# A recorded two-block transformer kernel: exact shapes in its planner, an order by latest start time, and weight slots of 4352 bytes

## The chip, the cores and the metric

The kernel runs on one core of a Trainium2 chip. The metric is the device time of one execution in microseconds, lower is better. TensorE (PE) multiplies, with its weight loads on a path of their own (PEld); VectorE (DVE), ScalarE (ACT) and GpSimd (POOL) do elementwise work; SyncE (SP) starts the DMA transfers. Each engine works off its own list of instructions in order, and waits where an input or a buffer isn't ready.

## The reference, cut to what matters

Two blocks follow one another on 512 tokens of width 1024, in float32.

```python
def reference(x, ...):
    x = first_block(...)     # rmsnorm; h @ w_in; mLSTM, pooling and memory-attention branches, each
                             # times silu of a gate; concatenated @ w_out; rmsnorm
    return second_block(...)

def second_block(...):       # h is 512 x 1024
    p = h @ w_in + b_in
    a_u, a_v, q, k, v, r, a_low, g_a, g_b = split(p)
    y_a = spatial_gating(a_u, a_v, ...)
    log_f = log_sigmoid(a_low @ gla_w_gate2 + gla_b_gate) / 16
    o = gla_chunked(q, k, v, log_f)          # gated linear attention, 4 heads, below
    y_b = normalise(o) * gla_norm_g * silu(r)
    m = sigmoid(g_a) * y_a + sigmoid(g_b) * y_b
    h = layer_norm(alpha * h + m @ w_out)
    f = square(relu(h @ w_ff1)) @ w_ff2      # 1024 -> 4096 -> 1024
    return layer_norm(alpha * h + f)

def gla_chunked(q, k, v, log_f):             # per chunk of 64 tokens, with a state carried over
    cum = cumsum(log_f)
    scores[t, s] = sum_d q[t, d] * k[s, d] * exp(cum[t, d] - cum[s, d])   for s <= t
    out = scores @ v + (q * exp(cum)) @ state
```

## The kernel before, in words

**Weights.** All big products are taken in the format fp32r, with three matmuls in place of one: activations and weights are each split into a high and a low part, and high·high, high·low and low·high are added up in PSUM. The weights come as 184 chunks of 128x1024 numbers or close to it, numbered in the order in which they are used. A chunk n is loaded by an SP DMA into a tile `wr`n; ACT copies it, rounded, into `wh`n; DVE takes the difference `wl`n = `wr`n − `wh`n (`split_to`, L562 to 577). Tiles `wr`, `wh` and `wl` have four buffers each (`RAW, HL = 4, 4`, L541). A chunk then feeds 24 matmuls of 128x512 into one PSUM bank (`fm`, L637, through `mm3`, L506: two with `wh`, one with `wl`, eight times): the weight is the stationary side, and the moving side is a page `pg` of activations (512 tokens x 4 bytes). In eight chunks (56 to 63, the `av` columns) the sides are changed: 48 matmuls whose moving side is 256 columns of the weight (`units_tok`, L650). Some chunks (117 to 123, and most of the second feed-forward matrix) are put into pages `pg` instead of `wh` and `wl`; they are called paged. Inside a chunk the eight input pages are gone through in turn, so the first matmul with `wl` is the third of the chunk.

**Recording and planning.** Nothing is issued when the Python code runs. `Recorder.add` (L142) notes every operation with its tiles and what it depends on; `costs` (L185) gives each a modelled time by its engine, its kind and the number of elements n that its views (`View`, L62) report. `serial` (L236) makes an order in which the tiles fit in their buffers; `order` (L286) is a list scheduler over the five engines: at each step it takes for each engine, among the operations whose inputs are planned, the one that can start first, looking through them in program order, and of the engines' candidates the one with the earliest start. `issue` (L413) then emits everything, so every instruction of the profile carries one line, L431. The last line of the kernel calls `rec.issue(rec.order({...}))`.

A view keeps n exactly only while it is a plain slice. After a `rearrange` followed by an index it reports the n of the whole tile: a 128x4x32 part of a `big` tile of 768 columns is costed with n = 768.

**The GLA stage.** While the chunks from about 82 to 104 (the `q`, `k`, `r` and `ga` columns of the second block's input product) are multiplied, the function `gla` (L1431) lays the attention's work beside them. For each of four heads and each of five levels, DVE and POOL build decayed copies of q and k in `big` and `pg` tiles, PE makes small score products (`score`, L1527, into banks such as `ps751`, `ps752`), and DVE copies their valid triangles out of PSUM with COPY_PREDICATED into one page (such as `pg721`). Beside this, DVE takes each finished chunk out of its PSUM bank (`pg760<-ps750,pg486`: bank plus bias page), applies a product with an activation's result (SCALAR_TENSOR_TENSOR), and makes the next `wl`. So DVE's list mixes three kinds of rows: those that need a PE result, those that prepare the next scores, and the weight splits. In the order rows below, `ps719`, `ps731`, `ps741`, `ps750`, `ps762` and `ps776` are the banks of chunks 93, 94, 95, 96, 97 and 98; the numbers behind the underscores count the recorded rows.

Of the kernel before, what the change touches and what calls it, by code (L numbers as in the profile page):

```python
# [1 line left out]

# [5 lines left out]
F32 = mybir.dt.float32  # L8
F32R = mybir.dt.float32r
# [12 lines left out]
SLOT = 1088  # L22
# [23 lines left out]
class Tile_:  # L46


    def __init__(self, pool, shape, dtype, tag, bufs, nm):
        self.pool, self.shape, self.dtype, self.tag, self.bufs, self.nm = pool, list(shape), dtype, tag, bufs, nm  # L50
        self.real = None
        self.psum = tag == "ps"
        n = 1
        for s in shape[1:]:
            n *= s
        self.cols = n
        self.writes, self.reads = [], []
        self.first = self.last = None
        self.left = 0


class View:  # L62
    def __init__(self, tile, steps=(), lo=0, hi=None, flat=None, rows=None, n=None, dt=None):
        self.tile, self.steps = tile, steps
        self.lo, self.hi = lo, tile.cols if hi is None else hi
        self.flat = len(tile.shape) == 2 if flat is None else flat
        self.rows = tile.shape[0] if rows is None else rows
        self.n = self.hi - self.lo if n is None else n
        self.dt = tile.dtype if dt is None else dt

    def _next(self, step, **kw):
        a = dict(lo=self.lo, hi=self.hi, flat=self.flat, rows=self.rows, n=self.n, dt=self.dt)
        a.update(kw)
        return View(self.tile, self.steps + (step,), **a)

    def __getitem__(self, ix):
        step = ("getitem", (ix,), {})
        whole = ix if isinstance(ix, tuple) else (ix,)
        if self.flat and all(isinstance(s, slice) and s.step is None for s in whole):
            rows = len(range(*whole[0].indices(self.rows)))  # L80
            lo, hi = self.lo, self.hi
            if len(whole) > 1:
                a, b, _ = whole[1].indices(self.hi - self.lo)
                lo, hi = self.lo + a, self.lo + b
            return self._next(step, lo=lo, hi=hi, rows=rows, n=hi - lo)
        return self._next(step, flat=False)

    def bitcast(self, dt):
        return self._next(("bitcast", (dt,), {}), dt=dt)

    def rearrange(self, p, **kw):
        return self._next(("rearrange", (p,), kw), flat=False)

    def unsqueeze(self, i):
        return self._next(("unsqueeze", (i,), {}), flat=False)

    def to_broadcast(self, shape):
        n = 1
        for s in shape[1:]:
            n *= s  # L100
        return self._next(("to_broadcast", (shape,), {}), flat=False, n=n)

    def real(self):
        ap = self.tile.real
# [25 lines left out]
class Recorder:  # L130
# [54 lines left out]
    def costs(self, o):  # L185

        kw, eng = o.kw, o.eng
        out = kw["out"]
        n = out.n if isinstance(out, View) else 512
        ins = [v for k, v in kw.items() if isinstance(v, View) and k not in WRITES]  # L190
        ps = any(v.tile.psum for v in ins)
        o.port, o.table, o.tail = False, None, 60
        if eng == "PE":
            o.tail = 230
            if o.what == "transpose":
                o.cost = 112
            else:
                n = kw["rhs"].n
                slow = kw["rhs"].dt == F32
                o.cost = 2 * max(112, 0.85 * n) if slow else max(113, 0.449 * n)  # L200
        elif eng == "ACT":
            extra = sum(isinstance(kw.get(k), View) for k in ("scale", "bias"))
            o.cost = (150 if ps else 190) + 0.835 * n + 95 * extra + (206 if "accum_out" in kw else 0)
            fn = kw["func"].name if hasattr(kw["func"], "name") else str(kw["func"]).rsplit(".", 1)[-1]
            o.table = EXACT.get(fn)
        elif eng == "DVE":
            n = max(n, max((v.n for v in ins), default=0))
            ptr = any(isinstance(kw.get(k), View) for k in ("scalar", "scalar1", "scalar2"))
            big = [k for k in ("in_", "in0", "in1", "data", "mask", "data0", "data1") if isinstance(kw.get(k), View)]
            sb = [k for k in big if not kw[k].tile.psum]  # L210
            o.port = len(sb) >= 2 or (len(sb) == 1 and len(big) == 1 and o.what in ("tensor_copy", "tensor_scalar"))
            o.cost = 140 + 1.045 * n + 65 * ptr
            if o.what == "memset":
                o.cost = 50 + n
            elif o.what == "tensor_scalar" and not ps and n >= 256:
                o.cost = 140 + 0.55 * n + 65 * ptr
            elif o.what == "copy_predicated":
                o.cost = 150 + 1.15 * n
            elif o.what == "tensor_tensor_scan":
                o.cost = 1800  # L220
            elif n <= 16:
                o.cost = 210
        elif eng == "POOL":
            o.port = o.what != "memset"
            o.cost = 190 + 2.15 * n
            if o.what == "memset":
                o.cost = 515
            elif o.what == "affine_select":
                o.cost = 260 + 0.75 * n
            elif o.what == "tensor_copy":  # L230
                o.cost = 200 + 1.3 * n
        else:
            o.cost = 440
            o.tail = 2100
# [48 lines left out]
                t.last = i  # L283
        self.ops = order

    def order(self, caps, window=1 << 30):  # L286
        import heapq
        import numpy as np
        self.serial(caps)
        ops = self.ops  # L290
        n = len(ops)
        tags = list(caps)
# [16 lines left out]
        pend = {e: [] for e in engines}  # L309
        for o in ops:  # L310
            o.waiting, o.ready, o.start = len(o.deps), 0.0, None
        for o in ops:
            if not o.waiting:
                heapq.heappush(pend[o.eng], o.i)
        head = 0
        port = 0.0
        wire = 0.0
# [44 lines left out]
        done = 0  # L362
        order = []
        while done < n:
# [6 lines left out]
            pend[e].remove(i)  # L371
            cost = o.cost
            if o.table and table not in o.table:
                table = o.table[0]
# [25 lines left out]
            for j in o.users:  # L400
                u = ops[j]
                u.ready = max(u.ready, o.end if u.eng != e else s + cost + (0 if e != "SP" else o.end - s - cost))
                u.waiting -= 1
                if not u.waiting:
                    pend[u.eng].append(j)
            while head < n and ops[head].start is not None:
                head += 1
            order.append(i)
# [35 lines left out]
def tile_two_blocks(ctx, tc, wa, wb, xT, memT, vec, cst, rows, poolw, wst, wg2, out):  # L444
    ctx.enter_context(tc.manual_schedule())
    rec = Recorder(tc.nc)
# [115 lines left out]
    def split_to(i):  # L562
        while n_sp[0] <= min(i, NCH - 1):
            c = n_sp[0]
            t = raw.pop(c)
            n = src[c].shape[1]
            if c in paged:
                h, l = Pair(), Pair()
                for i in range(2):
                    split(h.pages[i], l.pages[i], t[:, i * T:(i + 1) * T])  # L570
            else:
                h = rec.tile(sb, [128, n], F32R, tag="wh", name=f"wh{c}", bufs=HL)
                l = rec.tile(sb, [128, n], F32R, tag="wl", name=f"wl{c}", bufs=HL)
                split(h, l, t)
            wsp[c] = (h, l)
            n_sp[0] += 1
# [159 lines left out]
    first = []  # L736
    if True:
# [8 lines left out]
            G.memset(f(b), 0.0)  # L746

        for c in range(2):
            first.append([rec.tile(sb, [128, 1040], dt, tag=tag, name=f"{tag}{c}", bufs=n)
                          for tag, dt, n in (("wr", F32, RAW), ("wh", F32R, HL), ("wl", F32R, HL))])  # L750
            wsp[c] = first[c][1:]
        for k in range(8):
            s = slice((k % 4) * 260, (k % 4 + 1) * 260)
# [1384 lines left out]
```

## Time and profile before

| | us |
|---|---|
| time, median of 3 runs (lowest to highest) | 1162.99 (1160.61 to 1163.28) |
| the profiled execution's own time | 1163.84 |
| its span, first to last instruction | 1161.7 |
| PE busy | 1132.3 |
| DVE busy | 706.0 |
| ACT busy | 514.8 |
| POOL busy | 183.3 |
| mean granted TensorE clock over the span | 0.990 |

The span is the time between the first and the last instruction in the trace; the execution's own time is 2.1 us longer. A busy time is the sum over an engine's instructions with overlaps taken out. The granted clock is TensorE's clock as a share of full speed. In the profile, times on the axis are microseconds from the span's start.

### The profile page before, as it was taken

To read this page: it belongs to the slowest core of one execution; us is meant where nothing else is said; L and a number is where in the kernel's file an instruction comes from. 1 tells how busy PE (TensorE), PEld (TensorE's weight loads), DVE (VectorE), ACT (ScalarE), POOL (GpSimd) and SP (SyncE) were. 2 spreads that over 40 slices of the span, in tenths; PEclk is the share of its full clock that TensorE was granted. 3 is DMA by queue.
4 is the path that set the end of the run, shared out by engine and by line. 5 is a ranking of instruction groups with operands and counts; after the bars stand their busy time and mean duration, and the time that the engine had idled before them with its cause. 6 is when DMAs were issued, how large, how long until landed. Compare 5 with 4: busy or idle time off the path is not lost.

```text
span 1161.7 us, 15202 instructions
## 1 busy us (share of the span) xinstructions
PE 1132.3 (97%) x5808; PEld 957.3 (82%) x5808; DVE 706.0 (61%) x1291; ACT 514.8 (44%) x868; POOL 183.3 (16%) x244
## 2 busy tenths in 40 slices
PE   8999999999999999999998899998999999999997
PEld 8888888878889998888876777898888888888885
DVE  6878887886445665565665887887333336423334
ACT  7766535453334525854554343446232226222211
POOL 5112002000120000432444533001000000000005
PEclk9999999999999999999998999999999999999998
DMA  8324222522323222220221131340222223324201
GB/s 300 110 91 174 72 75 80 163 92 93 104 76 110 75 91 71 95 91 19 73 91 37 55 116 66 101 142 31 72 90 93 91 96 105 108 92 156 79 1 72
DMA packets 33799, 108.85 MB, mean 94 GB/s; under 512 B 3888, under 2 KB 5040, under 8 KB 33728
## 3 DMA queue, kind: packets, MB, share of 16 engines
q1 hardware_dynamic: 33728, 107.90, 27.8%
q8 instruction: 45, 0.74, 0.3%
q14 instruction: 26, 0.21, 0.1%
HBM read 105.79 MB, written 2.10 MB: 93 GB/s over the span
## 4 chain that ended last, share of the span: by engine, by line
PE 96%; DVE 3%; ACT 0%; DMA 0%; issue 0%; SPq 0%; DVEq 0%
PE ps L431 96%; DVE pg L431 1%; DVE wl L431 1%; DVE big L431 0%; DMA wr<-in_wb_dram 0%; ACT wh L431 0%; ACT pg L431 0%; DVE sm L431 0%; SPq L431 0%; DVEq L431 0%
## 5 line engine op out<-in xcount | busy, mean ns | idle before, releaser
L431 PE MATMUL ps<-pg,wh 128*128 128x512 f32 (+1 forms) x1952 | 602.7, 391 | 0.9 <-ACT wh L431 0.9
L431 PEld LDWEIGHTS ps<-pg,wh 128*128 128x128 f32 x1952 | 363.1, 189 | 77.7 <-ACT wh L431 1.3
L431 PE MATMUL ps<-pg,wl 128*128 128x512 f32 (+1 forms) x976 | 378.9, 389 | 7.9 <-DVE wl L431 7.7
L431 ACT ACTIVATE wh<-wr 128x1024 fp32r<-128x1024 f32 (+2 forms) x159 | 163.1, 1026 | 338.8 <-PE ps L431 300.6
L431 DVE TENSOR_TENSOR wl<-wr,wh 128x1024 fp32r<-128x1024 f32 (+1 forms) x151 | 189.6, 1258 | 160.9 <-ACT wh L431 160.8
L431 PE MATMUL ps<-pg,pg 128*128 128x512 f32 (+4 forms) x1280 | 241.1, 344 | 3.4 <-DVE pg L431 2.0
L431 PEld LDWEIGHTS ps<-pg,pg 128*128 128x128 f32 (+1 forms) x1280 | 207.4, 192 | 33.5 <-DVE pg L431 2.6
L431 PEld LDWEIGHTS ps<-pg,wl 128*128 128x128 f32 x976 | 184.3, 189 | 50.5 <-DVE wl L431 10.6
L431 POOL TENSOR_TENSOR pg<-pg,pg 128x128 f32<-128x128 f32 (+4 forms) x113 | 111.5, 995 | 654.1 <-ACT pg L431 565.4
L431 ACT ACTIVATE pg<-pg 128x512 fp32r<-128x512 f32 (+6 forms) x254 | 133.0, 550 | 106.4 <-DVE pg L431 91.7
L431 PE MATMUL ps<-wh,pg 128*128 128x260 f32 (+2 forms) x800 | 170.2, 308 | 5.4 <-ACT wh L431 5.4
L431 DVE TENSOR_TENSOR pg<-ps,pg 128x512 f32<-128x512 f32 (+4 forms) x153 | 95.1, 630 | 82.0 <-PE ps L431 76.5
L431 DVE TENSOR_TENSOR pg<-pg,pg 128x512 f32<-128x512 f32 (+7 forms) x207 | 124.2, 623 | 32.1 <-ACT pg L431 14.0
L431 PEld LDWEIGHTS ps<-wh,pg 128*128 128x128 f32 x800 | 130.6, 191 | 12.8 <-ACT wh L431 5.4
L431 PE MATMUL ps<-wl,pg 128*128 128x260 f32 (+2 forms) x400 | 121.3, 305 | 0.0
L431 PEld LDWEIGHTS ps<-wl,pg 128*128 128x128 f32 x400 | 76.0, 190 | 3.9 <-issue 0.5
L431 DVE TENSOR_TENSOR pg<-wr,pg 128x512 fp32r<-128x512 f32 x62 | 40.8, 689 | 61.8 <-issue 41.5
L431 ACT ACTIVATE pg<-wr 128x512 fp32r<-128x512 f32 x62 | 35.4, 623 | 83.4 <-PE ps L431 75.7
L431 DVE SCALAR_TENSOR_TENSOR pg<-pg,pg 128x512 f32<-128x512 f32 (+3 forms) x76 | 51.4, 693 | 4.7 <-ACT pg L431 4.2
L431 ACT ACTIVATE pg<-ps 128x512 f32<-128x512 f32 (+5 forms) x78 | 39.8, 529 | 21.1 <-PE ps L431 20.3
L431 ACT ACTIVATE pg<-pg,vt 128x512 f32<-128x512 f32 (+3 forms) x60 | 39.0, 655 | 10.9 <-DVE pg L431 9.9
L431 DVE SCALAR_TENSOR_TENSOR pg<-pg,vt,pg 128x512 fp32r<-128x512 f32 (+4 forms) x48 | 37.3, 788 | 5.8 <-ACT pg L431 5.0
(131 smaller groups left out, 537.6 us busy)
## 6 DMA issues: line engine op xcount, KB each, us to landing
wr<-in_wa_dram SPq DMA_DIRECT2D x172, 512.0 KB, 3.5
wr<-in_wb_dram SPq DMA_DIRECT2D x10, 520.0 KB, 3.5
pg<-in_xT_dram SPq DMA_DIRECT2D x16, 256.0 KB, 4.1
pg<-in_rows_dram SPq DMA_DIRECT2D x10, 256.0 KB, 4.1
out_dram<-pg SPq DMA_DIRECT2D x8, 256.0 KB, 2.0
wr<-in_wb_dram SPq DMA_DIRECT2D x8, 130.0 KB, 4.0
pg<-in_memT_dram SPq DMA_DIRECT2D x4, 256.0 KB, 7.4
pg<-in_wst_dram SPq DMA_DIRECT2D x2, 256.0 KB, 3.9
```

What stands on the lines that cost most here:

```text
L431: getattr(real[o.eng], o.what)(**kw)
```

## The change

**Exact shapes.** `View` carries its `shape` through indexing, `rearrange`, `unsqueeze` and broadcasts, and n is worked out from it. The modelled costs of the DVE's and POOL's parts of the GLA stage change with it. Three cost constants change too.

**The planner's priority.** `order` now runs the scheduler (`schedule`, the old loop) six times. The first time the priority is program order as before. After each round, `latest` walks the plan backwards and gives each operation the latest time at which it can start without delaying the plan's end, through the operations that use its result, and through PE's own sequence of that plan; the next round looks through candidates by that time. The plan with the earliest modelled end is issued.

**The weight slots.** All `wh` and `wl` tiles get `SLOT` = 1088 columns, 4352 bytes (before 1040 columns, 4160 bytes, the largest of the tiles that share the slots). Chunks of the kinds `km` (4 chunks), the eight `av` chunks and chunk 116 are put 16, 48 and 16 columns into their slot.

The built programs have the same instructions for computing: 5808 recorded matmuls and transposes on PE, 1291 on DVE, the same table loads on ACT. By the addresses in the built programs, `wh` starts 177952 bytes into a partition in both; `wl` starts at 194592 before and 195360 now; the pages `pg` start at 30240 and are 2048 bytes apart. Modulo 256 all pages stand at 32. The four slots of `wh` and of `wl` stand at 32, 96, 160 and 224 before (4160 = 16·256 + 64) and all at 32 now (4352 = 17·256).

```diff
     def __getitem__(self, ix):
...
+        shape = []
+        for k, d in enumerate(self.shape):
+            if k >= len(whole):
+                shape.append(d)
+            elif isinstance(whole[k], slice):
+                shape.append(len(range(*whole[k].indices(d))))
...
-        return self._next(step, flat=False)
+        return self._next(step, flat=False, shape=shape)
...
             elif o.what == "copy_predicated":
-                o.cost = 150 + 1.15 * n
+                o.cost = 160 + 1.1 * n
             elif o.what == "tensor_tensor_scan":
-                o.cost = 1800
+                o.cost = 1200
             elif n <= 16:
-                o.cost = 210
+                o.cost = 165
...
-    def order(self, caps, window=1 << 30):
+    def order(self, caps, rounds=6):
+
+
+        self.serial(caps)
+        got = None
+        prio = [float(o.i) for o in self.ops]
+        for _ in range(rounds):
+            order = self.schedule(caps, prio)
+            if got is None or self.end < got[0]:
+                got = self.end, order, [(o.start, o.end) for o in self.ops]
+            prio = self.latest()
...
+    def latest(self):
+        ops = self.ops
+        end = self.end
+        seq = sorted(ops, key=lambda o: -o.start)
+        late = [end] * len(ops)
+        pe = end
+        pos = {o.i: k for k, o in enumerate(seq)}
+        for o in seq:
+            t = end
+            for j in o.users:
+                t = min(t, late[j] - (o.cost if ops[j].eng == o.eng else o.cost + o.tail))
+            t = min(t, end - o.cost)
+            if o.eng == "PE":
+                t = min(t, pe - o.cost)
+                pe = t
+            late[o.i] = t
+        return late
+
+    def schedule(self, caps, prio):
...
-            for i in sorted(pend[e]):
-                if i > head + window:
-                    break
+            for _, i in pend[e]:
...
+    shift = {4 + i: 16 for i, w in enumerate(ORDER1) if w[0] == "km"}
+    shift.update({4 + len(ORDER1) + 12 + i: 48 for i in range(8)})
+    shift[4 + len(ORDER1) + 12 + 16 + len(ORDER2) + 4] = 16
...
-                h = rec.tile(sb, [128, n], F32R, tag="wh", name=f"wh{c}", bufs=HL)
-                l = rec.tile(sb, [128, n], F32R, tag="wl", name=f"wl{c}", bufs=HL)
+                o = shift.get(c, 0)
+                h = rec.tile(sb, [128, SLOT], F32R, tag="wh", name=f"wh{c}", bufs=HL)[:, o:o + n]
+                l = rec.tile(sb, [128, SLOT], F32R, tag="wl", name=f"wl{c}", bufs=HL)[:, o:o + n]
```

Outside the GLA stage the two orders differ by local swaps. Inside it, two places show the difference.

DVE, GLA stage, before: the rows that lead up to the split of chunk 98.

```order
L431 TENSOR_TENSOR pg746_5839<-pg654_5195,pg746_5839 128x512
L431 COPY_PREDICATED pg721_5616<-ct_180,ps751_5960 128x4x24 x2
L431 COPY_PREDICATED pg721_5616<-ct_180,ps751_5960 128x4x16 x2
L431 COPY_PREDICATED pg721_5616<-ct_180,ps751_5960 128x4x8 x2
L431 COPY_PREDICATED pg721_5616<-ct_180,ps752_5963 128x4x24 x2
L431 COPY_PREDICATED pg721_5616<-ct_180,ps752_5963 128x4x16 x2
L431 COPY_PREDICATED pg721_5616<-ct_180,ps752_5963 128x4x8 x2
L431 TENSOR_TENSOR pg774_6003<-ps762_5914,pg486_3575 128x512
L431 SCALAR_TENSOR_TENSOR pg748_5856<-pg749_5863,pg748_5856 128x512
L431 TENSOR_TENSOR wl98_6008<-wr98_5713,wh98_5799 128x1024
```

DVE, the same place now: the rows that lead up to the split of chunk 98.

```order
L500 TENSOR_TENSOR wl97_5797<-wr97_5493,wh97_5778 128x1024
L500 SCALAR_TENSOR_TENSOR pg729_5782<-pg730_5788,pg729_5782 128x512
L500 TENSOR_TENSOR pg746_5801<-pg654_5207,pg746_5801 128x512
L500 TENSOR_TENSOR pg739_5827<-ps731_5776,pg486_3575 128x512
L500 COPY_PREDICATED pg721_5613<-ct_180,ps732_5823 128x256
L500 COPY_PREDICATED pg721_5613<-ct_180,ps732_5823 128x128
L500 COPY_PREDICATED pg721_5613<-ct_180,ps733_5833 128x256
L500 COPY_PREDICATED pg721_5613<-ct_180,ps733_5833 128x128
L500 TENSOR_TENSOR gsq_5637<-gsq_5637,ps738_5839 4x512
L500 SCALAR_TENSOR_TENSOR pg739_5827<-pg740_5850,pg739_5827 128x512
L500 TENSOR_TENSOR wl98_5872<-wr98_5598,wh98_5825 128x1024
```

Before, `wl98` stood behind the row that reads `ps762`, the bank of chunk 97; now the latest chunk's bank that a row ahead of it reads is `ps731`, that of chunk 94.

PE, GLA stage, before: the end of chunk 96 and what follows it.

```order
L431 MATMUL ps750_5867<-pg462_3347,wh96_5626 128x512
L431 MATMUL ps750_5867<-pg461_3309,wl96_5775 128x512
L431 MATMUL ps762_5914<-pg437_3050,wh97_5758 128x512
L431 MATMUL ps762_5914<-pg438_3057,wh97_5758 128x512
L431 MATMUL ps776_5920<-pg437_3050,wh98_5799 128x512
L431 MATMUL ps776_5920<-pg438_3057,wh98_5799 128x512
L431 MATMUL ps795_5924<-pg437_3050,wh99_5854 128x512
L431 MATMUL ps795_5924<-pg438_3057,wh99_5854 128x512
L431 MATMUL ps762_5914<-pg437_3050,wl97_5933 128x512
L431 MATMUL ps762_5914<-pg439_3062,wh97_5758 128x512
```

PE, the same place now.

```order
L500 MATMUL ps750_5911<-pg462_3347,wh96_5677 128x512
L500 MATMUL ps750_5911<-pg461_3309,wl96_5685 128x512
L500 MATMUL ps751_5969<-big745_5843,pg746_5801 128x192 x2
L500 MATMUL ps752_5978<-big745_5843,pg746_5801 128x192 x2
L500 MATMUL ps762_5986<-pg437_3050,wh97_5778 128x512
L500 MATMUL ps762_5986<-pg438_3057,wh97_5778 128x512
L500 MATMUL ps762_5986<-pg437_3050,wl97_5797 128x512
L500 MATMUL ps762_5986<-pg439_3062,wh97_5778 128x512
```

Before, PE took the first two matmuls of the chunks 97, 98 and 99, those that need no `wl`, ahead of the first `wl97`; now the chunks run whole, one behind the other, with the scores (`ps751`, `ps752`) between two of them.

## Rows read from the trace of the kernel before

**Rows 1.** The page: busy time, share and instructions by engine; chain that ended last.

```profile
PE 1132.3 (97%) x5808; PEld 957.3 (82%) x5808; DVE 706.0 (61%) x1291; ACT 514.8 (44%) x868; POOL 183.3 (16%) x244
...
PE 96%; DVE 3%; ACT 0%; DMA 0%; issue 0%; SPq 0%; DVEq 0%
```

**Rows 2.** PE's waits, whole span: us in total, times, longest us.

```profile
PE ps L431 <- ACT wh L431: 6.3, 2, 5.4
```

**Rows 3.** PE's waits, 551 to 671 us, the GLA stage.

```profile
PE ps L431 <- DVE wl L431: 7.7, 6, 2.6
PE ps L431 <- DVE pg L431: 3.1, 2, 2.0
```

**Rows 4.** Stretches: us; busy (instructions) PE, PEld, DVE, ACT, POOL; PEclk; DMA share; GB/s.

```profile
551.00:580.00 29.00, 27.94 (x136) 23.45 (x135) 20.55 (x63) 16.02 (x37) 11.74 (x18) 1.00 0.22 73
...
610.00:640.00 30.00, 25.41 (x102) 20.15 (x101) 17.67 (x52) 11.96 (x29) 14.40 (x27) 0.89 0.11 36
...
sum 120.00, PE 107.42 PEld 87.61 DVE 83.96 ACT 57.97 POOL 53.90; mean PE 26.86 PEld 21.90 DVE 20.99 ACT 14.49 POOL 13.48
```

**Rows 5.** Timeline, 612 to 632 us: start, us, instruction [idle before, releaser].

```profile
615.40 0.69 DVE L431 TENSOR_TENSOR pg<-ps,pg 128x512 f32<-128x512 f32 x1 [4.29 <-PE ps L431]
616.01 0.68 DVE L431 SCALAR_TENSOR_TENSOR pg<-pg,pg 128x512 f32<-128x512 f32 x1
...
616.61 1.22 DVE L431 TENSOR_TENSOR wl<-wr,wh 128x1024 fp32r<-128x1024 f32 x1
...
617.74 1.73 DVE L431 TENSOR_TENSOR big<-pg,big 128x384 f32<-128x384 f32 x3
...
617.88 0.50 PE L431 MATMUL ps<-pg,wl 128*128 128x512 f32 x1 [1.12 <-DVE wl L431]
...
619.40 0.68 DVE L431 TENSOR_TENSOR pg<-pg,pg 128x512 f32<-128x512 f32 x1
...
622.56 1.75 DVE L431 COPY_PREDICATED pg<-ct,ps 128x96 f32<-128x96 uint32 x12 [2.48 <-PE ps L431]
...
624.69 0.69 DVE L431 TENSOR_TENSOR pg<-ps,pg 128x512 f32<-128x512 f32 x1 [0.38 <-PE ps L431]
...
627.17 0.80 PE L431 MATMUL ps<-pg,wl 128*128 128x512 f32 x1 [2.62 <-DVE wl L431]
...
629.05 1.06 PE L431 MATMUL ps<-pg,wh 128*128 128x512 f32 x2
...
630.33 1.06 PE L431 MATMUL ps<-pg,wh 128*128 128x512 f32 x2
```

**Rows 6.** Stretches of four feed-forward chunks in a row, PE alone.

```profile
882.88:888.32 5.44, 5.44 (x25) 1.00 0.28 96
888.32:893.82 5.50, 5.50 (x25) 1.00 0.30 98
893.82:899.36 5.54, 5.54 (x25) 1.00 0.30 95
899.36:904.91 5.55, 5.55 (x26) 1.00 0.27 94
```

**Rows 7.** Stretches of four `av` chunks, one in each slot, PE alone.

```profile
341.85:347.60 5.75, 5.75 (x50) 1.00 0.01 3
347.60:353.06 5.46, 5.46 (x51) 1.00 0.58 178
377.36:383.06 5.70, 5.70 (x51) 1.00 0.32 99
383.06:388.70 5.64, 5.64 (x50) 1.00 0.30 94
```

**Rows 8.** Stretch of the layer norm behind `w_out`, PE alone.

```profile
788.00:815.00 27.00, 24.58 (x168) 0.87 0.07 21
```

More of the change, by code (lines that the diff above doesn't have):

```diff
@@ L1 @@
+from bisect import insort
 from collections import deque
@@ L62, with __init__ @@
 class View:
-    def __init__(self, tile, steps=(), lo=0, hi=None, flat=None, rows=None, n=None, dt=None):
+    def __init__(self, tile, steps=(), lo=0, hi=None, flat=None, rows=None, shape=None, dt=None):
         self.tile, self.steps = tile, steps
         self.lo, self.hi = lo, tile.cols if hi is None else hi
+        self.shape = tuple(tile.shape) if shape is None else tuple(shape)
         self.flat = len(tile.shape) == 2 if flat is None else flat
         self.rows = tile.shape[0] if rows is None else rows
-        self.n = self.hi - self.lo if n is None else n
+        self.n = 1
+        for d in self.shape[1:]:
+            self.n *= d
         self.dt = tile.dtype if dt is None else dt
     def _next(self, step, **kw):
-        a = dict(lo=self.lo, hi=self.hi, flat=self.flat, rows=self.rows, n=self.n, dt=self.dt)
+        a = dict(lo=self.lo, hi=self.hi, flat=self.flat, rows=self.rows, shape=self.shape, dt=self.dt)
         a.update(kw)
@@ L84, in __getitem__ @@
                 lo, hi = self.lo + a, self.lo + b
-            return self._next(step, lo=lo, hi=hi, rows=rows, n=hi - lo)
-        return self._next(step, flat=False)
+            return self._next(step, lo=lo, hi=hi, rows=rows, shape=shape)
+        return self._next(step, flat=False, shape=shape)
     def bitcast(self, dt):
@@ L91, in rearrange, with groups @@
     def rearrange(self, p, **kw):
-        return self._next(("rearrange", (p,), kw), flat=False)
+        size = dict(kw)
+        left, right = [side.replace("(", " ( ").replace(")", " ) ").split() for side in p.split("->")]
+        def groups(words):
+            got, deep = [], None
+            for w in words:
+                if w == "(":
+                    deep = []
+                elif w == ")":
+                    got.append(deep)
+                    deep = None
+                elif deep is None:
+                    got.append([w])
+                else:
+                    deep.append(w)
+            return got
+        for d, names in zip(self.shape, groups(left)):
+            known, open_ = 1, None
+            for w in names:
+                if w in size:
+                    known *= size[w]
+                else:
+                    open_ = w
+            if open_:
+                size[open_] = d // known
+        shape = []
+        for names in groups(right):
+            d = 1
+            for w in names:
+                d *= size[w]
+            shape.append(d)
+        return self._next(("rearrange", (p,), kw), flat=False, shape=shape)
     def unsqueeze(self, i):
-        return self._next(("unsqueeze", (i,), {}), flat=False)
+        return self._next(("unsqueeze", (i,), {}), flat=False, shape=self.shape[:i] + (1,) + self.shape[i:])
     def to_broadcast(self, shape):
[L98 to L101, printed above, removed]
+        return self._next(("to_broadcast", (shape,), {}), flat=False, shape=shape)
     def real(self):
@@ L284, in serial @@
         self.ops = order
-    def order(self, caps, window=1 << 30):
+    def order(self, caps, rounds=6):
[7 more added lines that the diff above has]
+            prio = self.latest()
+        self.end = got[0]
+        for o, (s, e) in zip(self.ops, got[2]):
+            o.start, o.end = s, e
+        return got[1]
+    def latest(self):
[16 more added lines that the diff above has]
+    def schedule(self, caps, prio):
         import heapq
         import numpy as np
-        self.serial(caps)
         ops = self.ops
@@ L370, in order @@
             o = ops[i]
[L371 removed]
+            pend[e].remove((prio[i], i))
             cost = o.cost
@@ L748, in tile_two_blocks @@
         for c in range(2):
[L749 to L750 removed]
+            first.append([rec.tile(sb, [128, w], dt, tag=tag, name=f"{tag}{c}", bufs=n)
+                          for tag, dt, n, w in (("wr", F32, RAW, 1040), ("wh", F32R, HL, SLOT), ("wl", F32R, HL, SLOT))])
             wsp[c] = first[c][1:]
```

4 lines of the change are left out of this document (2 added, 2 removed).

## Prediction

> **What bounds the kernel now.** I read the page's busy times and its chain first. PE is busy for 1132.3 us of a span of 1161.7, and the chain of waits that ended last is 96% PE and 3% DVE [rows 1]. So there are two ways to gain: take away PE's idle time, some 29 us, or make PE's matmuls themselves follow each other faster. Idle time of the other engines is worth nothing.
>
> Then I asked what PE waits for. 5.4 us are the head, in which the first weight is loaded and split [rows 2]; the change leaves the first rows of SP, ACT and DVE as they were, so that stays. The largest lump behind it lies in the GLA stage, 551 to 671 us. There PE is busy for 107.42 of 120 us: 12.58 us idle [rows 4]. 7.7 of these are six waits for a `wl`, 3.1 two waits for a page that DVE makes [rows 3]. The timeline shows how such a wait comes about. At 615.40 DVE, which had itself waited 4.29 us for PE, takes a finished chunk out of PSUM (0.69), multiplies (0.68), and only then makes the `wl` of the next chunk (1.22), while PE stands still; the same again at 624.69, where PE waits 2.62 us [rows 5]. DVE isn't short of time on the whole (83.96 of 120 us [rows 4]); it waits for PE, and then PE waits for it. The split stands in DVE's list behind the row that reads the chunk before.
>
> The second wait has a sequel: from 627.17 on three matmuls take 1.28 us (629.05 to 630.33 [rows 5]), where 24 take 5.44 in an undisturbed stretch [rows 6], 0.68 for three. The stretch's granted clock is 0.89 [rows 4]: PE ran at 1.2 GHz for a while after the waits. A clock of half for x of 30 us with a mean of 0.89 gives x = 6.6 us, so 3.3 us lost; counted by matmuls, some 13 at 427 ns for 227, it is 2.6.
>
> Last, the pace where PE never waits. Four feed-forward chunks in a row, 24 matmuls each, at full clock and without idle time, take 5.44, 5.50, 5.54 and 5.55 us [rows 6], and each following group of four chunks repeats it. The weight slots are four. The fast one is the slot that stands at 32 modulo 256 like the pages. The `av` chunks show the same kind of thing with other signs: 5.75, 5.46, 5.70 and 5.64 [rows 7].
>
> **Part 1: the slots' pace.** Now all slots stand where the fast one stood. The mean of the four is 5.508, so a chunk gains 0.066 us [rows 6]. 116 chunks have a weight in a slot as stationary side and 512 moving columns: 116 x 0.066 = 7.7 us. The clean stretches are those of the feed-forward part; elsewhere matmuls of other kinds stand between the chunk's own, and fewer neighbours gain. No row gives that share: I take a fifth off, 6.2, and for the low end a third, 5.1. The eight `av` chunks go to what the 5.46 slot has (48 columns are 192 bytes, the same place relative to the pages): mean 5.64 less 5.46, times 8, is 1.4 [rows 7]. The first eight chunks of the second feed-forward matrix also use slots: 8 x 0.066 = 0.5. The four `km` chunks and chunk 116 have no clean row: 0. Sum 8.1, I take **8.0**; ends 5.4 (the low end of the first term, and little from the others) and 9.9 (everything in full, and a few tenths from the `km` chunks). All of it lies on PE, which is the path.
>
> Here the Trainium skill speaks against this part: its page "SBUF — State Buffer", section "Who interferes with whom", gives PE two independent read ports, one for the moving operand and one for the weight load, and says that PE never waits on anyone. By it the place of a slot couldn't matter and this term would be 0. The four stretches differ by up to 2% with the slot alone, so I go by them; the rule is a rival below.
>
> **Part 2: DVE's order in the GLA stage.** I counted for each split how many PE matmuls stand between the latest PE result that a DVE row ahead of it reads and the first matmul that uses it. That is the time by which DVE can be late. Before, it is 0 to 8 for the chunks 89, 97 to 100 and 102. Now it is 93, 88, 90, 65, 65 and 81, the smallest of the stage being 65: at 0.227 us each about 15 us. The order rows show it for chunk 98: behind the bank of chunk 97 before, behind that of 94 now. So the pattern at 615 and 624 us can't come again in that form, and 7.7 us of waits for `wl` and the 3.1 for pages lose their cause.
>
> What is late next is DVE itself. Between `wl98` and `wl99` its list now has six products into `big` (3.5), two bank rows (1.4), 24 copies (3.5 at the rate of the twelve at 622.56), two SCALAR_TENSOR_TENSOR (1.4), one page (0.7) and the split (1.2): 11.7 us [rows 5], against 7 to 8 us of PE for a chunk with its scores. From chunk 98 to 102 this adds up to 47 us of DVE against 32 of PE: DVE falls behind by 15. The lead of `wl102` is 81 matmuls, 18 us. That covers it, with 3 us to spare, less than a tenth of the sum; the tightest score row has a lead of 6 us of PE over 3.4 of DVE. So I keep 2 us of the 12.58 and take **10.6**; ends 0 (the DVE rival) and 12.6.
>
> PE's new order costs nothing by itself: the matmuls are the same in number and kind, and a whole chunk in sequence is what rows 6 show at full pace.
>
> **Part 3: the clock.** Without waits of 1 and 2.6 us some 10 us apart the clock has no cause to fall at 627. I take 2.6, ends 0 and 3.3 [rows 4, 5].
>
> **The rest.** The costs by exact shape, `latest` and the three constants act only through the order. Outside the GLA stage rows are swapped locally. The dearest other place, the layer norm behind `w_out`, has 2.42 us idle and a clock of 0.87 [rows 8] and keeps nearly its order: between −0.3 and +0.3, taken as 0. SP moves two late loads behind a weight load; four `wr` buffers hide that, and if they didn't, a load's few us would show as a PE wait once. POOL's work moves ahead within the stage, where it is busy for 53.90 of 120 us [rows 4]: 0.
>
> **Sum.** 8.0 + 10.6 + 2.6 = 21.2 us. The profiled execution took 1163.84, so 1142.6; the median of the runs is 0.85 below that execution, so I say **1142**. The forecast's own range: gains of 5.4 + 7 + 0 to 9.9 + 12.6 + 3.3, that is 1151 to 1137.
>
> **Rivals.**
> - DVE becomes the bound of the chunks 98 to 102. For it: 11.7 us against 7 to 8 a chunk. Against: the lead, and 83.96 busy of 120 us over the stage. Then some 8 of the 12.6 us come back, and with such waits the clock's fall: gain 8.0 + 4.6, time **1150 to 1151**.
> - The pace doesn't follow the slots' place: the period of four is then something else that goes along with the slot, for instance which bank or buffer it meets, and the new addresses change nothing. For it: only one set of addresses was run. Against: the `av` chunks, with sides changed, have another fast slot, which the same relation of addresses gives. Gain 13.2, time **1150**. The Trainium skill's rule named above ("SBUF — State Buffer", "Who interferes with whom") is what would make it so.
> - The plan doesn't carry over and nothing moves: stalls come back at other rows and the pace stays. Time **1162**.
> - Slower: whole chunks in sequence leave PE nothing to fill a wait with. Before, it could take six matmuls of the next chunks that need no `wl`; now every late split stops it in full at its third matmul. Place: the chunks 87 to 92 and 98 to 104. If the lead isn't there when DVE enters them, its shortfall (4 + 15 us) shows in full as waits, 19 in place of 12.6, and each wait of 2 to 3 us lets the clock fall again at 2.6. Against the pace's gain of 8.0 the sign turns when the clock falls three times in place of once (6.4 + 2 x 2.6 = 11.6); with six falls the time is 1163 + 6.4 + 13 − 8 = **1174**.
>
> **How the numbers follow.** The forecast has 0.78, DVE as the bound 0.08, no pace 0.07, nothing moves 0.03, slower 0.04. A measurement of this kernel tells about 0.3% from no change, 3.5 us, so the first three count as faster (0.93), the fourth as same. The range must leave out no more than 0.2: it takes in the forecast's range and the two rivals at 1150, up to 1152.
>
> **What would show it.** Pace right: four feed-forward chunks in a row all take 5.44, and each `av` chunk 5.46. Order right: PE idle over the GLA stage 1 to 4 us, DVE's own waits for PE there fewer, a granted clock of 1.00 in each of its stretches. DVE the bound: waits of PE for `wl` or `big` around the chunks 100 to 104, with DVE busy without a gap ahead of them. I am wrong if the feed-forward chunks still differ with period four, or if PE still waits more than 8 us in the stage.

## The result, and the profile after

The changed kernel takes **1136.74 us** (median of 4 runs, 1136.0 to 1137.25) against 1162.01 for the kernel before, measured with it: a ratio of 0.9782, 95% interval 0.9765 to 0.9799, that is 25.3 us less. The forecast was 1142 with a range of 1137 to 1152. The direction and the two main causes, pace and order, were right; the time lies 5.3 us below the forecast and 0.3 below its range. About 1.0 of the 5.3 is the kernel before itself, whose median was 1162.99 when the forecast was made; the gain is 25.3 where the sum had 21.2.

The page of the changed kernel, its busy times and its chain, which answer to [rows 1]:

```profile
PE 1117.9 (99%) x5808; PEld 954.4 (84%) x5808; DVE 710.1 (63%) x1291; ACT 515.8 (45%) x868; POOL 183.6 (16%) x244
...
PE 98%; DVE 1%; ACT 0%; DMA 0%; issue 0%; SPq 0%
```

PE's busy time fell by 14.4 us, and the span, 1134.7 after 1161.7, by 27.0: the other 12.6 us are idle time. PE's waits over the whole span of the changed kernel (us in total, times, longest us):

```profile
PE ps L500 <- ACT wh L500: 5.5, 1, 5.5
PE ps L500 <- ACT pg L500: 2.9, 4, 1.5
```

Every wait of [rows 3] is gone; the head [rows 2] and the layer norm behind `w_out` are left. The GLA stage, from the first matmul of chunk 84 to that of chunk 112 and cut at the chunks 96 and 104, first of the kernel before, then of the changed one (stretch, us, busy of PE, PEld, DVE, ACT, POOL, granted clock, DMA share, GB/s):

```profile
516.00:609.58 93.58, 89.88 (x426) 75.06 (x426) 61.04 (x164) 48.15 (x94) 36.16 (x60) 1.00 0.19 63
609.58:660.31 50.73, 44.97 (x198) 36.68 (x198) 34.09 (x105) 19.67 (x44) 24.21 (x48) 0.93 0.13 42
660.31:734.76 74.45, 71.33 (x322) 56.42 (x321) 60.47 (x96) 31.70 (x52) 26.75 (x17) 1.00 0.25 85
sum 218.76, PE 206.19 PEld 168.15 DVE 155.61 ACT 99.52 POOL 87.13; mean PE 68.73 PEld 56.05 DVE 51.87 ACT 33.17 POOL 29.04
```

```profile
513.60:601.93 88.33, 88.33 (x427) 75.27 (x426) 68.02 (x170) 48.96 (x97) 35.11 (x65) 1.00 0.23 78
601.93:664.23 62.30, 62.30 (x305) 53.16 (x303) 56.13 (x142) 30.72 (x64) 33.20 (x45) 1.00 0.20 63
664.23:712.38 48.15, 48.15 (x218) 38.28 (x217) 32.55 (x50) 19.11 (x25) 11.25 (x8) 1.00 0.21 73
sum 198.78, PE 198.78 PEld 166.71 DVE 156.70 ACT 98.79 POOL 79.56; mean PE 66.26 PEld 55.57 DVE 52.23 ACT 32.93 POOL 26.52
```

The stage went from 218.76 to 198.78 us, 20.0 of the 27.0. PE has no idle time in it at all, with the same DVE work, 156.70 us for 155.61. Four feed-forward chunks in a row of the changed kernel, which answer to [rows 6], and the first two of the last four `av` chunks, 60 to 63, which answer to [rows 7], PE alone (the rows left out read 5.44 too):

```profile
857.78:863.22 5.44, 5.44 (x26) 1.00 0.29 99
863.22:868.66 5.44, 5.44 (x26) 1.00 0.30 99
868.66:874.10 5.44, 5.44 (x26) 1.00 0.30 96
...
```

```profile
363.88:369.32 5.44, 5.44 (x50) 1.00 0.32 97
369.32:374.76 5.44, 5.44 (x50) 1.00 0.30 95
...
...
```

The period of four is gone, as forecast. Of the `av` chunks only these last four are at 5.44; the first ones take 5.65, as the experiment on the shifts shows.

### The profile page after: what moved, and what is told of

Its sections match the earlier page's. It is cut to its first block, busy times and chain, and to the rows that moved or that the text cites. A ratio compares the mean times of both kernels' runs of the same rounds, so it can differ in the third digit from the quotient of the medians.

```text
span 1134.7 us, 15224 instructions
## 1 busy us (share of the span) xinstructions
PE 1117.9 (99%) x5808; PEld 954.4 (84%) x5808; DVE 710.1 (63%) x1291; ACT 515.8 (45%) x868; POOL 183.6 (16%) x244
## 4 chain that ended last, share of the span: by engine, by line
PE 98%; DVE 1%; ACT 0%; DMA 0%; issue 0%; SPq 0%
PE ps L500 98%; DVE pg L500 0%; DMA wr<-in_wb_dram 0%; ACT pg L500 0%; DVE sm L500 0%; ACT wh L500 0%; DVE wl L500 0%; SPq L500 0%; ACT bhl L500 0%
## 5 line engine op out<-in xcount | busy, mean ns | idle before, releaser
L500 DVE SCALAR_TENSOR_TENSOR pg<-pg,pg 128x512 f32<-128x512 f32 (+4 forms) x76 | 54.8, 739 | 4.5 <-ACT pg L500 4.0
L500 ACT ACTIVATE pg<-ps 128x512 f32<-128x512 f32 (+5 forms) x78 | 39.7, 529 | 12.7 <-PE ps L500 12.2
```

The lines of the kernel that those rows point to most:

```text
L500: getattr(real[o.eng], o.what)(**kw)
```

## The experiments

The times of kernels are medians. Each stands beside the kernel before on the same chip, whose medians were 1161.1 to 1161.2. The mean granted clock of a run tells how often it fell: in a run in which it falls only behind the last matmuls it is 0.997, and 0.001 less is up to 1.1 us of span.

### Which half brings what: slots and order apart

The changed kernel's order with the old slots:

```diff
-                h = rec.tile(sb, [128, SLOT], F32R, tag="wh", ...)[:, o:o + n]
+                h = rec.tile(sb, [128, 1040], F32R, tag="wh", ...)[:, o:o + n]
...
-    shift = {4 + i: 16 for i, w in enumerate(ORDER1) if w[0] == "km"}
+    shift = {}
```

> The changed kernel's order with the slots of before (1040 columns, 4160 bytes, no shifts). Theory A, pace goes with the slots' place modulo 256: the feed-forward chunks fall back to 5.44, 5.50, 5.54 and 5.55 us, the av chunks to 5.75, 5.46, 5.70 and 5.64; PE has no more waits than the changed kernel; 1136.7 + 10.3 = 1147. Theory B, the pace came with the order or with the waits that went: all chunks stay at 5.44, the time at 1137.

1143.44 us, ratio 0.9838 (0.9823 to 0.9854). The four feed-forward chunks of this kernel:

```profile
860.54:865.98 5.44, 5.44 (x25) 1.00 0.27 99
865.98:871.48 5.50, 5.50 (x25) 1.00 0.31 98
871.48:877.02 5.54, 5.54 (x26) 1.00 0.30 95
877.02:882.56 5.54, 5.54 (x25) 1.00 0.25 95
```

The pattern of before is back, so it came from the slots and from nothing in the order. There are no waits in the GLA stage, which takes 200.33 us. Beside the kernel before (1161.2) the order alone is worth 17.8 us. The total is 3.6 us better than theory A's 1147, for which the runs' clock can account: 0.997 in three of four, where the changed kernel has 0.993 to 0.995.

The opposite half, the kernel before with the new slots:

```diff
-                h = rec.tile(sb, [128, n], F32R, tag="wh", name=f"wh{c}", bufs=HL)
+                o = shift.get(c, 0)
+                h = rec.tile(sb, [128, SLOT], F32R, tag="wh", name=f"wh{c}", bufs=HL)[:, o:o + n]
```

> The kernel before with the new slots and shifts alone; its order is unchanged. Theory A: pace gain 10.3, so 1162.0 - 10.3 = 1151.7, and PE's waits in the GLA stage stay at 12 us or grow by the time that PE gains there (about 1 us). Theory B: no gain, 1162. If the two gains don't add up, the rest of the 25.3 us is in what the two do together.

1153.2 us, ratio 0.9925 (0.9909 to 0.994): the slots alone bring 8.0. PE's waits for `wl` are those of before:

```profile
PE ps L431 <- DVE wl L431: 7.8, 6, 2.6
...
PE ps L431 <- DVE pg L431: 3.1, 2, 2.0
```

Its GLA stage, cut as above but in one piece (us, busy of PE, PEld, DVE, ACT, POOL, granted clock, DMA share, GB/s):

```profile
512.59:727.11 214.52, 201.84 (x944) 166.01 (x942) 155.50 (x363) 99.55 (x188) 87.03 (x124) 1.00 0.20 67
```

So with the waits of before, 12.7 us of idle time, the clock stayed at its full level through the stage in this execution. At the same slots and the same clock the new order takes 198.78: it is worth 15.7 us there.

17.8 and 8.0 make 25.8, about the whole of 25.3. To see how the clock mixes in I ran the old slots once more, beside the changed kernel's program (the one-round kernel below, the same order row by row).

> The changed kernel's order with the slots of before, once more, beside the changed kernel's program. The first time 1143.4 in the median, with hardly any fall of the clock in its runs (mean granted clock 0.997 in three of four, 0.993 to 0.995 in the changed kernel's). Theory A, the pace is worth 9 us by itself and the falls of the clock come and go: 1143 to 1147, and spans at like clocks differ by 9. Theory B, with slots at one place the clock falls oftener, so part of the gain is given back: clocks of 0.997 here and 0.993 to 0.995 in the one-round kernel once more, and the difference of the medians stays at 6.5.

1143.21 against 1137.12: the slots are worth 6.1 us here. The granted clock was 0.996 or 0.997 in all five of these runs with the old slots (0.995 in one of the four above) and 0.993 or 0.994 in all runs of the other. Theory B holds in this: with the new slots the clock fell oftener. 0.003 of the clock is 3.4 us, so as an estimate the slots are worth about 9.5 at a like clock, near theory A's 9, and a third of it was given back. The stretches in which the clock fell, first of the changed kernel, then of the old slots, and last one of them of the kernel with the scale of places (next section), PE alone:

```profile
450.00:455.00 5.00, 5.00 (x21) 0.91 0.17 70
455.00:460.00 5.00, 5.00 (x12) 0.50 0.02 5
460.00:465.00 5.00, 5.00 (x21) 0.91 0.32 105
785.00:790.00 5.00, 4.65 (x26) 0.66 0.01 3
```

```profile
450.00:455.00 5.00, 5.00 (x25) 1.00 0.29 86
455.00:460.00 5.00, 5.00 (x21) 1.00 0.05 21
460.00:465.00 5.00, 5.00 (x23) 1.00 0.12 23
785.00:790.00 5.00, 4.05 (x29) 1.00 0.00 0
```

```profile
455.00:460.00 5.00, 5.00 (x24) 1.00 0.09 19
```

Around 455 us PE is busy without a gap in all three, and yet it ran at 1.2 GHz for 6.8 us in one. The scale of places is the same program as the changed kernel up to chunk 124, at some 794 us, so neither the slots nor the order settle by themselves whether the clock falls there; the profiled executions differ. The kernel before, with the old slots, fell there too, for 3.4 us. What decides it was not tested.

### The shifts, and a scale of places

```diff
-    shift = {4 + i: 16 for i, w in enumerate(ORDER1) if w[0] == "km"}
...
+    shift = {}
```

> The changed kernel without the shifts (all chunks at column 0 of a 4352-byte slot). Theory A, the pace goes with the place of the stationary side relative to the moving side modulo 256: the eight av chunks go from 5.46 us to that of place 0, 5.75, and the four km chunks and chunk 116 lose about 0.1 each; 512-wide chunks stay: 1136.7 + 8 x 0.29 + 0.5 = 1139.5. Theory B, only the alike slots count and not the shifts: 1137.

1137.99 us. The same `av` chunks without their shift, two of four alike:

```profile
364.98:370.74 5.76, 5.76 (x50) 1.00 0.30 92
370.74:376.50 5.76, 5.76 (x50) 1.00 0.31 92
...
...
```

So with the weight as the moving side and the page as the stationary one, place 0 is slow, 5.76, and 192 bytes further is faster. But there the pace has two levels. Chunk 56, the first of the eight, in the changed kernel, and chunk 60 in the order of the last round (below), both shifted by 192 bytes and with nothing else among their 48 matmuls:

```profile
339.77:345.42 5.65, 5.65 (x50) 1.00 0.01 3
```

```profile
367.16:372.81 5.65, 5.65 (x51) 1.00 0.32 94
```

In the changed kernel chunks 56 and 57 take 5.65 and 60 to 63 take 5.44; the step comes inside chunk 59, at 358.2 us, behind one small matmul of another kind, from 118 to 113 ns a matmul. In the order of the last round all six stay at 5.65. So here the place isn't all, and what picks the level was not tested. The eight chunks together take 45.99 us with the shift and 47.83 without, 1.8 less. The total moved by 1.3 us where 2.8 were expected, which is within its interval of 1.7 us either way.

```diff
+    steps = (0, 1, 2, 4, 8, 12, 16, 24, 32, 40, 48, 52, 56, 60)
+    shift.update({124 + i: steps[i // 2] for i in range(28)})
```

> The changed kernel with the 28 feed-forward chunks 124 to 151 put 0, 1, 2, 4, 8, 12, 16, 24, 32, 40, 48, 52, 56 and 60 columns (4 bytes each) into their slot, two chunks each; the order is the same. Theory A: a chunk's time follows its shift: 5.44 us at 0, 5.55 at 16 columns (64 bytes), 5.53 at 32 (128), 5.50 at 48 (192), as the four slots of before; what lies between them is not known. The time is 28 x 0.06 = 1.7 us above the changed kernel's, 1138.5. Theory B: all chunks stay at 5.44.

1138.93 us. Feed-forward chunks with shifts of 0, 32, 64, 128, 192 and 240 bytes, PE alone:

```profile
799.18:804.63 5.45, 5.45 (x26) 1.00 0.27 96
840.00:845.60 5.60, 5.60 (x25) 1.00 0.27 94
862.40:868.00 5.60, 5.60 (x26) 1.00 0.30 97
884.83:890.40 5.57, 5.57 (x26) 1.00 0.26 94
907.19:912.69 5.50, 5.50 (x25) 1.00 0.31 95
940.52:946.00 5.48, 5.48 (x25) 1.00 0.33 118
```

One program, one order, and the pace of 24 matmuls follows the shift alone. Shifts of 48, 96, 160, 208 and 224 bytes take 5.57 to 5.62; none of 32 bytes and more is as fast as 0, and at 4 to 16 bytes other matmuls stand among the chunk's or just ahead of them. It isn't a matter of 64-byte steps: a chunk shifted by 32 bytes takes as long as one shifted by 64. Nor is it smooth: 240 and 192 are close to 0, and 224 between them is not. Only the weight was moved; the pages stayed where they were.

### Which part of the planner made the order

One round in place of six, so that the priority by latest time is never used:

```diff
-    def order(self, caps, rounds=6):
+    def order(self, caps, rounds=1):
```

> The changed kernel with one round of planning in place of six: priority in program order alone, with exact shapes and the new cost constants. Its order is the changed kernel's row by row on all five engines, so every theory expects the changed kernel's time, 1136.7; it stands here as the changed kernel beside the other three on one chip.

1137.12 us, as the changed kernel. So the order by latest time, which the title names, isn't in the changed kernel's program: the planner keeps the plan with the earliest modelled end, and that was the first round's. The order of the last round, issued in its place:

```diff
-            if got is None or self.end < got[0]:
+            if got is None or prio[0] != 0.0:
```

> The changed kernel, with the plan of the last of the six rounds issued in place of the one with the earliest modelled end (which is that of the first round, in program order: with one round alone the planner gives the same order row by row). So this is the order by latest start time that the change names. Theory A, the exact shapes did it and the priority matters little: splits have leads of 88 to 155 matmuls, no waits in the GLA stage, 1136 to 1139. Theory B, work put off to its latest time leaves no room for errors of the modelled costs: new waits of some us, 1140 to 1150.

1137.57 us.

> The changed kernel with the last round's order, once more, beside the first round's (the one-round kernel). Theory A, the two orders are worth the same: within 1.5 us of each other. Theory B, the room that it has more at the splits 100 to 104 (leads 93 to 155) or the page waits that it has more make a difference: over 2 us either way.

1138.15 us beside 1137.12 of the first round's: the two orders are worth the same within about a microsecond. The other way round, the priority by latest time without the exact shapes:

```diff
-        return self._next(step, flat=False, shape=shape)
+        return self._next(step, flat=False)
...
-                o.cost = 160 + 1.1 * n
+                o.cost = 150 + 1.15 * n
```

> The changed kernel with the views and cost constants of before (a rearranged part counts with the n of its whole tile), but with the six rounds, the priority by latest time and the new slots. Here the planner takes the third round's order. Splits 89 and 100 have leads of 11 and 4 matmuls, 101 of 26, the others 50 or more. Theory A, exact shapes are what removes the waits: waits of 4 to 10 us in the GLA stage, 1142 to 1148. Theory B, the priority by latest time does as much by itself: under 3 us of waits, 1137 to 1140.

1177.01 us, ratio 1.0128 (1.0111 to 1.0144): slower than the kernel before, although it has the new slots. Both theories were wrong here. PE's waits over the span:

```profile
PE ps L463 <- DVE pg L463: 20.4, 13, 5.4
PE ps L463 <- ACT wh L463: 5.9, 1, 5.9
PE ps L463 <- DVE big L463: 4.2, 1, 4.2
```

A likely reading, which no run shows by itself, is that a priority that puts work off to the last moment by wrong costs makes it late. What the runs show is that the exact costs removed the waits (shapes and the three constants together; they were not tried apart): with the new slots and program order as the priority, the old costs give 1153.2 us and the waits above, the exact ones 1137.1 and none. With the exact costs the priority hardly matters; with the old ones it costs some 24 us, 1177.0 for 1153.2.

### Is it the splits' place in DVE's list?

The kernel before, with seven splits moved up behind its planner, once as far as their buffer allows, once by about one chunk:

```diff
+    for c in (89, 97, 98, 99, 100, 101, 102):
+        mine = ...                     # the DVE split of chunk c
+        plan.remove(mine)
+        plan.insert(at, mine)          # behind the last use of wl(c - 4) / ahead of the bank row of chunk c - 2
```

> The kernel before with one change behind its planner: the weight splits of chunks 89 and 97 to 102 are moved up in DVE's list to behind the last use of the wl buffer that they take; everything else stays, slots too. Theory A, the waits come from the split that stands behind the bank row: PE's 7.7 us of waits for wl go, and the fall of the clock at 627 us with them (2.9): 1162 - 10.6 = 1151, with the waits for pages left (3.1). Theory B, DVE is short of time there whatever stands first: each split that is ahead delays bank rows and score copies by 1.2 us, the waits move to pages and big tiles, and the time stays within 3 us of 1162.

1160.99 us, ratio 0.9998 (0.9983 to 1.0013): no change. Part of a gain may be hidden, since the clock fell oftener in most of its ten runs (0.990 to 0.991 in the median, against 0.993); the profiled execution, at 0.994, took 1157.85. PE's waits in the stage, and then DVE's:

```profile
PE ps L431 <- DVE pg L431: 6.0, 4, 3.2
PE ps L431 <- DVE big L431: 2.9, 1, 2.9
...
PE ps L431 <- DVE wl L431: 0.6, 1, 0.6
```

```profile
DVE pg L431 <- PE ps L431: 10.8, 10, 1.8
DVE pg L431 <- ACT pg L431: 10.3, 7, 4.7
DVE wl L431 <- ACT wh L431: 9.2, 5, 3.4
```

The waits for `wl` went from 7.7 to 0.6, as theory A has it. But the splits now stand so early that DVE waits 9.2 us for ACT's `wh`, which itself waits for PE, and the scores queue behind: page and `big` waits rise from 3.8 to 8.9 us, as theory B has it.

> The kernel before with the splits of chunks 89 and 97 to 102 moved up in DVE's list by about one chunk (ahead of the row that reads the bank two chunks back), in place of the three to four chunks of the kernel with the splits far ahead, where DVE stood waiting for ACT's wh. Leads 32 to 58 matmuls. Theory A, a lead of one or two chunks is enough: PE's 7.7 us of waits for wl go, other waits stay at 4.7; with the clock at its full level for the whole span the time would be 1147 to 1150, the median 1150. Theory B, DVE is short of time there in the order of before and what is gained for the splits is lost for scores: waits for pages and big tiles of 6 us or more, median 1155 to 1161.

1155.88 us, ratio 0.9935 (0.991 to 0.996), its fastest run at 1151.07 with a clock of 0.997. Waits for `wl` 0.6, for pages 3.4, for `big` 1.8: the stage, 218.76 us before, takes 210.2. That is about half of what the whole order gives in the stage; in the medians it is 5.4 of 17.8. So theory A holds for the splits themselves, whose waits go. The median lies where theory B had it, with page and `big` waits of 5.2 us in place of 3.8. The rest must lie in other rows that the exact costs move, the scores and bank rows; they were not moved by themselves.

### How much room DVE has left

```diff
+    for c in (98, 99, 100, 101, 102):
+        mine = ...                     # the place of the DVE split of chunk c in the plan
+        plan[mine:mine] = [plan[mine]] * 2
```

> The changed kernel with the splits of chunks 98 to 102 made three times over (ten more DVE instructions of 1.22 us, 12.2 us in all; the result is the same), order otherwise unchanged. In the changed kernel the smallest time from the end of a split to its first use is 7.6 us, at chunk 103, down from 21 at chunk 96. Theory A, DVE works off its list there with a reserve of that size: PE waits 12.2 - 7.6 = 4.6 us, 1141 to 1143 with a fall of the clock. Theory B, DVE has far more room, since it waits for PE in between: no wait, 1137. Theory C, the scores have less room than the splits: 8 us or more, 1145 and above.

1140.2 us, some 3.5 above the changed kernel's 1136.74, which ran on another chip. The waits of PE in the stage:

```profile
PE ps L500 <- DVE pg L500: 3.7, 3, 2.1
```

In size that is theory A's: 3.7 us of waits where 4.6 were expected of 12.2 us more DVE work. In place it is theory C's: the bank and score pages were late, not the splits, whose smallest time ahead of their use is still 5.9 us. The changed kernel has little more room than that because DVE itself hardly waits there. Its waits in that kernel from 602 to 664 us, 6.2 us in all, of which the added work leaves 0.6:

```profile
DVE pg L500 <- PE ps L500: 3.2, 3, 1.5
DVE pg L500 <- POOL pg L500: 1.8, 1, 1.8
DVE pg L500 <- ACT pg L500: 0.6, 2, 0.3
DVE big L500 <- ACT big L500: 0.6, 1, 0.6
```

## Why the prediction was right or wrong, point by point

**What bounds.** Right: PE was the path, and the gain came from its waits in the GLA stage and from its pace.

**The slots' pace, 8.0 (5.4 to 9.9).** Right in cause and about right in size: alone 8.0, behind the new order 6.1, and by the estimate above about 9.5 at a like clock. If that estimate holds, the discount of a fifth for chunks among other work was too large, but falls of the clock took more than that back. That the slots alone gave just the 8.0 forecast is in part luck: the `av` term came out at 0.9 us, not 1.4 (46.85 us for the eight chunks before, 45.99 now), since only the last half of them reached the fast level. Nor do the `av` chunks follow the same relation of addresses, as the second rival has it: they are slowest at place 0, where the feed-forward chunks are fastest. The Trainium skill's page "SBUF — State Buffer", section "Who interferes with whom", gives PE two independent read ports and says that PE never waits on anyone. It speaks of engines and ports and not of places; that a slot's place couldn't matter was my reading of it, and this kernel refutes that reading: one chunk takes 5.45 to 5.62 us with its place alone.

**The order's waits, 10.6 (0 to 12.6): the term that failed by size.** The order alone is worth 18.4 us of the stage: 218.76 to 200.33 with the old slots. Of these about 2.9 are the clock: from 627.17 to 633.57 us fifteen matmuls, not some 13, take 6.40 us, where the usual pace gives 3.45. That leaves 15.5. With the new slots and no fall of the clock it is 15.7, 214.52 to 198.78, and in the medians 16.1 (1153.2 to 1137.1). Two steps were too small. First, I kept 2 us of waits; none is left. Second, I took PE's idle time, 12.58 us, for the whole loss. A wait costs more than the idle time that is shown. The wait at 617.88 of the kernel before:

```profile
615.20 1.56 PE L431 MATMUL ps<-pg,wh 128*128 128x512 f32 x6
...
618.22 0.63 PE L431 MATMUL ps<-pg,wh 128*128 128x512 f32 x2
```

The last of the six starts five paces of 0.23 behind 615.20, at 616.36; the next matmul starts at 617.88 [rows 5], 1.52 later where 0.23 is usual: 1.29 lost, though the row says 1.12, since the row counts the 0.40 us of the last matmul's own duration as busy, where the next one usually starts after 0.23. And the first matmul behind the wait takes 0.34 to the next start, 0.11 more than usual. The stage's ten waits of over half a microsecond add up to 14.2 us from start to start less the pace, the restarts to about 0.7, and an eleventh, short wait to 0.3: 15.2 of the 15.5. The upper end of this term should have been 16, not 12.6.

**The clock, 2.6 (0 to 3.3).** Its cause isn't shown. Between the two profiled executions the clock gave about 3 us, 0.990 to 0.993, and the fall at 627 us is gone. But the kernel before with the new slots has the same waits in the stage and a granted clock of 1.00 there, so these waits don't always bring a fall; and the clock falls elsewhere, around 455 and 785 us, with the new slots oftener than with the old. In the medians little is left of this term: the kernel before ran at 0.991 to 0.996, the changed one at 0.993 to 0.995. That the sum came near all the same is because this shortfall stands against the surplus of the order's term.

**DVE falls behind by 15 us and the lead covers it.** Right. From chunk 96 to 103 the time from the end of a split to its first use shrinks from 21.4 to 7.6 us, by 14. The margin was larger than the 3 us that I gave it, and what ran out first with more work was the room of the pages, which the sum had priced only by one lead (6 us over 3.4).

**Whole chunks in sequence cost nothing; the rest 0.** Right: the stage runs without a gap.

**The cause named for the order.** I worked from the orders' rows and didn't ask which part of the planner had made them. The planner's six rounds and its latest times changed nothing; the exact costs did.

**The rivals.** "DVE becomes the bound" and "the pace doesn't follow" are refuted by the stage without waits and by the scale of places. "Slower" didn't come. In the kernel with latest times and the old shapes, which takes 1177, an order does make PE wait, but for pages (20.4 us) and `big` (4.2) and hardly for splits (0.9), by which that rival had it.

**The range.** The lower end, 1137.2, had all gains in full, 25.8, taken from the earlier median of 1162.99. The measured gain, 25.3, is inside that; from 1162.01 the same sum gives 1136.2. So the 0.3 us by which the time lies below the range is the kernel before's median, and within its noise. The fault in the sum is larger than that: the order brought 15.5 to 16 where its upper end was 12.6, the cap being the idle time shown, and the clock brought next to nothing in the medians. The lower limit of 7 us for the order's term in the range was given without a reason.

## What to carry to other kernels

Size a removed wait of PE from the start of the matmul before it to the start of the one behind it, less the usual pace, and add the restart: here 15.5 us for 12.6 of shown idle time. A list scheduler is as good as its costs: right element counts and constants were worth 16 to 18 us here, a cleverer priority nothing with them and a loss of some 24 without. When equal chunks of work differ with the buffer that they use, try the buffers' addresses before anything else.

## What the runs showed of the hardware that I had not expected

The pace of matmuls with a weight load each depends on the weight's place modulo 256 bytes, with the pages held at one place: 24 matmuls of 512 columns take 5.44 us at shift 0, 5.48 at 240, 5.50 at 192, and 5.57 to 5.62 at eight other shifts from 32 to 224. Slots 17·256 bytes apart are alike. Since no page was moved, it isn't shown that only the distance of the two operands counts. With the sides changed and 256 columns, 48 matmuls take 5.76 at 0; at 192 they take 5.65 or 5.44, and can pass from one to the other within a chunk.

The granted clock fell to 1.2 GHz in stretches in which PE had no idle time, around 455 us: for 6.8 us in the changed kernel's profiled execution, for 3.4 in the kernel before's, and not at all in that of the scale of places, which is the same program up to there. In the GLA stage it fell in the kernel before's profiled execution and not in that of the same order with new slots, with the same waits. The cause stays open.
